# One margin, two passes and small random ranks in the list scheduler of a decoder block (gMLP gate, Conformer convolution, SwiGLU)

## The chip, the cores and the metric

The kernel runs on one core of a Trainium2 chip. The metric is the device time of one execution in microseconds (us), as the median of several runs. Lower is better.

## What is computed

One decoder block on 1024 tokens of width 1024, in float32, ends in a modulated RMSNorm:

```python
def reference(x, c, ...):
    c_act = jax.nn.silu(c)
    cond = c_act @ ada_w[i] + ada_b[i]          # six vectors: shift, scale, gate, twice
    h = modulate(rmsnorm(x, norm1_g[i]), shift1, scale1)
    u, v, val, gate = jnp.split(h @ w_in[i] + b_in[i], ...)
    y_a = spatial_gating_mixer(gelu(u), gelu(v), ...)      # causal within chunks of 128
    y_b = conformer_conv_mixer(val, gate, ...)             # 31 taps, group norm, silu
    y = jnp.concatenate([rmsnorm(y_a, ...), rmsnorm(y_b, ...)], axis=-1)
    x = x + gate1 * (y @ w_out[i])
    h2 = modulate(rmsnorm(x, norm2_g[i]), shift2, scale2)
    g_ff, up_ff = jnp.split(h2 @ w_ffn_in[i], 2, axis=-1)
    x = x + gate2 * ((jax.nn.silu(g_ff) * up_ff) @ w_ffn_out[i])
    return modulate(rmsnorm(x, norm_f_g), shift_f, scale_f)
```

## The kernel before

**Tiling.** Features lie on the 128 partitions, tokens on the free axis, in two halves of 512 tokens (half 0 and half 1). A matrix operand is split into a high and a low part (`wh_`, `wl_` for weights, the two planes of `h`), and `mm3` (L750 to L752) multiplies high by high, low by high and high by low, 128x512 each. The feed-forward products (L1139) do the same, in a seven-product scheme on blocks (names A, B and C for the accumulators).

**Stages on TensorE.** The projections of half 0 (`p`, `pu`), then of half 1 (`p10_0`, `p11_0`), the projection v of half 0 (`v0_0` to `v0_3`) and of half 1 (`v1_`), with the group norm (`gn`) and the gate of the mixer (`pm`) of half 0 in between, the rest of half 1, the output projection (`po`), products of the feed-forward made ahead (`ah`), and then the feed-forward up and down to the final norm.

**What the other engines do meanwhile.** VectorE (DVE) runs the depthwise convolution tap by tap into two PSUM banks: L1073 begins one (`cv`), L1070 adds a tap, L1079 adds the sum to `s`. It also makes the conditioning columns: L703 multiplies one 128x1024 piece of `ada_w` by the activated c and sums it (ada23 is such a piece, `ada_1041` in the order below; ada36 to ada39 are later ones). GpSimd (POOL) makes the low parts of weights (L734), other pieces of the conditioning (L700, with the sum at L701 on ScalarE) and adds taps that ScalarE has multiplied (L1065).

**Places that the prediction names.**
- L858 and L860: TensorE sums the spatial weights into the PSUM bank `rs`, and four DVE instructions at L860 read it into `bst`. `rs` is one of three banks with the tag `mm`; `v0_0` takes it next, so TensorE's first L750 of `v0_0` waits for the last L860.
- L1101, L687, L1114, L1115: the group norm. A reciprocal (L1101), four DVE instructions at L687 that spread it on a diagonal (`gd`; L684 on ScalarE before them), two matmuls (L1114), and the product at L1115 on DVE. gd00 is the one of the first pair of channel blocks of half 0, gd01 that of the second pair.
- L1013, L1017, L1019: the mixer. Eight small matmuls each for `pm0_0` to `pm0_3` and `pm1_0` to `pm1_3`; DVE finishes each at L1017 and L1019. These use the two banks with the tag `gn`, so `pm1_0` and `pm1_1` wait for L1115 of the second pair, and `pm1_2` waits for L1019 of `pm1_0`.
- L795, L799, L805: sums of squares, their reciprocal root and its broadcast (`ssq_a0`, `rt_a0`; `ssq_b0`, `rt_b0`).
- L1242 to L1247, L1267 to L1281, L1131 and L1132: preparing the feed-forward's operands.

**What sets the order.** `block_kernel` writes the program once. At its end, `fix_order` (L561) reads all instructions, and a list scheduler decides the order of each engine's instructions; the order is then fixed by dependencies without semaphores between neighbours. Each engine runs its list strictly in that order. `duration` (L144) has a duration for each instruction, `Clock` (L337) a model of the engines, the DMA queue, TensorE's clock and one shared port of DVE and POOL. `forward` (L397) walks through time and gives each free engine the ready instruction of the lowest rank; `backward` (L456) does the same from the end and gives each step its tail, the time from its start to the end of the program; the negative tail is the rank of the next forward pass. `stretched` multiplies the durations of steps off TensorE by the first number of a margin, and the bytes of transfers by the second. Before, three margins with four rounds of backward and forward give twelve orders. `replay` runs a given order through the same model; `jittered` does so with durations that are stretched at random, and `fix_order` keeps the order with the smallest sum of four such replays.

Of the kernel before, what the change touches and what calls it, by code (L numbers as in the profile page):

```python
# [67 lines left out]
ENGINES = ("PE", "DVE", "Activation", "Pool", "SP")  # L68
SIGNAL = {"PE": 0.043, "DVE": 0.024, "Activation": 0.024, "Pool": 0.068, "SP": 0.05}
# [5 lines left out]
DMA_AHEAD = 0.5  # L75
SHORT_ROWS = 1.15
CLOCK_WINDOW = 3.4133
MARGINS = ((1.01, 1.05), (1.015, 1.075), (1.02, 1.1))
JITTER = (0.008, 0.08)
TRIALS = 4  # L80


class Step:
# [313 lines left out]
def forward(g, rank):  # L397

    import heapq
    count = len(g.steps)  # L400
    need, at = [len(s.before) for s in g.steps], [0.0] * count
    done, order = [0.0] * count, {e: [] for e in ENGINES}
    ready, waiting = ({e: [] for e in ENGINES} for _ in range(2))
    parked = {tag: [] for tag in g.order}
    slots, clock, table = Slots(g), Clock(True), None

    def arrive(n):
        tag, t = slots.blocked_on(g.steps[n])
        if tag is not None:
            parked[tag].append(n)  # L410
            return
        heapq.heappush(waiting[g.steps[n].engine], (max(at[n], t), n))

    def wake(tags):
        for tag in tags:
            again, parked[tag] = parked[tag], []
            for n in again:
                arrive(n)

    for s in g.steps:  # L420
        if not need[s.n]:
            arrive(s.n)
    for _ in range(count):
        t, e = pick(clock, ready, waiting)
        while waiting[e] and waiting[e][0][0] <= t + 1e-6:
            n = heapq.heappop(waiting[e])[1]
            heapq.heappush(ready[e], (rank[n], n))
        chosen = ready[e][0]
        if e == "Activation" and g.steps[chosen[1]].table not in (None, table):
            others = [x for x in ready[e] if g.steps[x[1]].table in (None, table)]  # L430
            if others and min(others)[0] < chosen[0] + TABLE_LOAD:
                chosen = min(others)
        ready[e].remove(chosen)
        heapq.heapify(ready[e])
        s = g.steps[chosen[1]]
        woken = slots.take(s)
        if s.table not in (None, table):
            table, t = s.table, t + TABLE_LOAD
        begin, end = clock.run(s, t)
        done[s.n] = end  # L440
        order[e].append(s)
        woken += slots.release(s, end + SIGNAL[e])
        woken += slots.hand_over() if woken else []
        wake(woken)
        for n in s.after:
            need[n] -= 1
            same = g.steps[n].engine == e and not s.dma
            if (s.n, n) in g.turns:
                at[n] = max(at[n], t + DMA_ISSUE)
            else:  # L450
                at[n] = max(at[n], (clock.free[e] if e == "PE" else end) if same else end + SIGNAL[e])
            if not need[n]:
                arrive(n)
    return order, done, slots.follows


def backward(g, rank, follows):

    import heapq
    count = len(g.steps)  # L460
    before = [sorted(s.before) for s in g.steps]
    need, at, tail = [len(s.after) for s in g.steps], [0.0] * count, [0.0] * count
    for old, new in follows:
        for n in g.first[new]:
            for m in g.final[old]:
                if m != n:
                    before[n].append(m)
                    need[m] += 1
    ready, waiting = ({e: [] for e in ENGINES} for _ in range(2))
    clock = Clock()  # L470
    for s in g.steps:
        if not need[s.n]:
            heapq.heappush(waiting[s.engine], (0.0, s.n))
    for _ in range(count):
        t, e = pick(clock, ready, waiting)
        while waiting[e] and waiting[e][0][0] <= t + 1e-6:
            n = heapq.heappop(waiting[e])[1]
            heapq.heappush(ready[e], (rank[n], n))
        s = g.steps[heapq.heappop(ready[e])[1]]
        if s.dma:  # L480
            begin = max(t, clock.queue)
            clock.queue = begin + s.bytes / (LOAD_RATE if s.load else STORE_RATE) + LOAD_GAP
            end = clock.queue - LOAD_GAP + (LOAD_WAIT if s.load else STORE_WAIT)
            clock.free[e] = t + DMA_ISSUE
        else:
            begin, end = clock.run(s, t)
        tail[s.n] = end
        for n in before[s.n]:
            need[n] -= 1
            other = g.steps[n].engine  # L490
            if (n, s.n) in g.turns:
                at[n] = max(at[n], begin + DMA_ISSUE)
                if not need[n]:
                    heapq.heappush(waiting[other], (at[n], n))
                continue
            at[n] = max(at[n], begin + s.issue - (s.finish - s.issue) if other == e == "PE" else end + SIGNAL[other])
            if not need[n]:
                heapq.heappush(waiting[other], (at[n], n))
    return tail


def replay(g, order):

    place, done, at = dict.fromkeys(ENGINES, 0), {}, [0.0] * len(g.steps)
    need = [len(s.before) for s in g.steps]
    slots, clock, table = Slots(g), Clock(True), None
    for _ in range(len(g.steps)):
        best = None
        for e in ENGINES:
            if place[e] == len(order[e]) or need[order[e][place[e]].n]:  # L510
                continue
            s = order[e][place[e]]
            tag, t = slots.blocked_on(s)
            t = max(t, at[s.n], clock.free[e])
            if tag is None and (best is None or t < best[0]):
                best = t, s
        t, s = best
        slots.take(s)
        if s.table not in (None, table):
            table, t = s.table, t + TABLE_LOAD  # L520
        begin, end = clock.run(s, t)
        done[s.n] = end
        if slots.release(s, end + SIGNAL[s.engine]):
            slots.hand_over()
        for n in s.after:
            need[n] -= 1
            if (s.n, n) in g.turns:
                at[n] = max(at[n], t + DMA_ISSUE)
            elif g.steps[n].engine == s.engine and not s.dma:
                at[n] = max(at[n], clock.free["PE"] if s.engine == "PE" else end)  # L530
            else:
                at[n] = max(at[n], end + SIGNAL[s.engine])
        place[s.engine] += 1
    return max(done.values())


@contextmanager
def stretched(g, factor):

    kept = [(s, s.issue, s.finish, s.port, s.dma and s.bytes) for s in g.steps if s.engine != "PE"]  # L540
    for s, issue, finish, port, size in kept:
        f = factor(s)
        if s.dma:
            s.bytes = size * f
        else:
            s.issue, s.finish, s.port = issue * f, finish * f, port * f
    yield
    for s, s.issue, s.finish, s.port, size in kept:
        if s.dma:
            s.bytes = size  # L550


def jittered(g, order, seed):

    import random
    rng = random.Random(seed)
    with stretched(g, lambda s: 1 + abs(rng.gauss(0, JITTER[s.dma]))):
        return replay(g, order)


def fix_order(tc, edges, stacked, reusing, rounds=4):  # L561

    g = Graph(list(tc.nc.cur_bb.bb.instructions), edges, stacked, reusing)
    orders = []
    for margin in MARGINS:
        with stretched(g, lambda s: margin[s.dma]):
            order, done, follows = forward(g, list(range(len(g.steps))))
            for _ in range(rounds):
                tail = backward(g, [-t for t in done], follows)
                order, done, follows = forward(g, [-t for t in tail])  # L570
                orders.append(order)
    times = [sum(jittered(g, order, seed) for seed in range(TRIALS)) for order in orders]
    best = orders[times.index(min(times))]
    for steps in best.values():
        for earlier, later in zip(steps, steps[1:]):
            tc.add_manual_dep(later.ins, earlier.ins.name,
                              mybir.DependencyInfo(mybir.DependencyClass.NoSync, mybir.DependencyReason.DATA),
                              reason="fix_order")
# [1067 lines left out]
```

## Time and profile before

| | us |
|---|---|
| median of 3 runs | 964.54 |
| lowest and highest run | 963.92, 966.73 |
| the profiled execution's own time | 967.9 |
| its span, first to last instruction | 965.8 |

The profiled execution is 3.4 us above the median, and 2.1 us of it lie outside the span. Times in rows below are counted from the span's start. In a timeline row stand the start, the duration (of the whole group where it ends in xN), the engine and line, the operation with output and inputs (buffer numbers left out) and, in brackets, the idle time before it and what ended that. In a table by windows stand the busy time of each engine and its instructions, the granted TensorE clock as a share of full speed (PEclk), and the DMA engines' share and rate.

### The profile page before, as it was taken

The page shows a single profiled execution, that of the slowest core. Times are in us where ns is not written, and L with a number is a line of the kernel's source. Part 1 is how long each engine was busy: PE and PEld are TensorE (multiplying, and loading weights), DVE is VectorE, ACT ScalarE, POOL GpSimd, SP SyncE. Part 2 cuts the span into 40 slices and gives each one's busy share as a digit, 9 for nine tenths or more (in the row PEclk, how much of TensorE's full clock was granted, in tenths as well). Part 3 has the DMA queues.
Part 4 walks back from the last instruction along what each step waited for, and adds up shares of the span by engine and source line. Part 5 has one row for each costly group of instructions (what it writes and reads, how often), then busy time and mean ns, then how long its engine had stood idle before and what let it go on. Part 6 is the DMA issues. An engine that isn't in the chain of part 4 may idle for free.

```text
span 965.8 us, 12863 instructions
## 1 busy us (share of the span) xinstructions
PE 946.5 (98%) x4461; PEld 767.1 (79%) x4461; DVE 861.9 (89%) x1226; ACT 482.1 (50%) x770; POOL 413.6 (43%) x253
## 2 busy tenths in 40 slices
PE   7999999999999999999999999999999999999996
PEld 4888777778777788887888888888888888888885
DVE  6989999999999763899999999999778989969966
ACT  6778468763474743554333333223337337227426
POOL 0069896776554403673545454554534200000132
PEclk9999999999999999999999999999999999999998
DMA  9873342443385443753677677767648848405104
GB/s 351 325 265 136 110 174 88 153 159 130 139 280 202 147 146 138 263 205 119 239 238 251 221 236 243 249 236 238 224 171 277 269 158 260 164 33 165 54 1 174
DMA packets 70498, 184.24 MB, mean 191 GB/s; under 512 B 7841, under 2 KB 8353, under 8 KB 70434
## 3 DMA queue, kind: packets, MB, share of 16 engines
q1 hardware_dynamic: 70434, 183.43, 55.0%
q8 instruction: 35, 0.57, 0.3%
q14 instruction: 29, 0.24, 0.1%
HBM read 142.24 MB, written 41.16 MB: 190 GB/s over the span
## 4 chain that ended last, share of the span: by engine, by line
PE 84%; DVE 9%; DMA 2%; ACT 2%; issue 2%; POOL 1%; SPq 0%; POOLq 0%; ACTq 0%; DVEq 0%
PE B L1139 31%; PE C L1139 18%; PE ah L1139 9%; PE A L1139 3%; PE po L752 3%; PE po L751 3%; PE po L750 3%; DVE cv L1070 2%; PE p L752 2%; PE p L750 2%; PE p L751 2%; PE v L750 2%; PE v L752 1%; DVE ada L703 1%; PE v L751 1%
## 5 line engine op out<-in xcount | busy, mean ns | idle before, releaser
L1139 PE MATMUL B<-h,w_f 128*128 128x512 f32 x816 | 189.9, 389 | 0.6 <-ACT w_f L1131 0.3
L1139 PEld LDWEIGHTS B<-h,w_f 128*128 128x128 f32 x816 | 153.1, 188 | 33.0 <-ACT w_f L1131 0.8
L1070 DVE SCALAR_TENSOR_TENSOR cv<-ypad,colt,cv 128x512 f32<-128x512 f32 x216 | 147.8, 745 | 0.3
L1139 PE MATMUL B<-fa,w_d 128*128 128x512 f32 x528 | 125.0, 389 | 0.0
L1139 PE MATMUL C<-h,w_f 128*128 128x512 f32 x528 | 123.7, 389 | 0.0
L1139 PEld LDWEIGHTS C<-h,w_f 128*128 128x128 f32 x528 | 99.1, 188 | 20.9 <-ACT w_f L1131 0.3
L1139 PEld LDWEIGHTS B<-fa,w_d 128*128 128x128 f32 x528 | 99.0, 188 | 20.9 <-DVE x L1500 0.3
L1139 PE MATMUL ah<-h,wh_a 128*128 128x512 f32 x320 | 101.3, 394 | 0.0
L1426 POOL TENSOR_TENSOR sq_nf<-sq_nf,sq_nf 128x512 f32<-128x512 f32 (+1 forms) x15 | 17.4, 1163 | 170.9 <-ACT sq_nf L1420 170.8
L1131 ACT ACTIVATE w_f<-raw_f 128x512 fp32r<-128x512 f32 x68 | 42.4, 630 | 87.8 <-PE B L1139 38.8
L734 POOL TENSOR_TENSOR wl_a<-raw_a,wh_a 128x1024 fp32r<-128x1024 f32 x20 | 49.4, 2468 | 77.0 <-ACT wh_a L733 77.0
L1131 ACT ACTIVATE w_d<-raw_d 128x512 fp32r<-128x512 f32 (+1 forms) x72 | 42.0, 593 | 80.2 <-PE B L1139 33.6
L1132 DVE TENSOR_TENSOR w_f<-raw_f,w_f 128x512 fp32r<-128x512 f32 x68 | 71.7, 1061 | 7.6 <-ACT w_f L1131 7.4
L1139 PEld LDWEIGHTS ah<-h,wh_a 128*128 128x128 f32 x320 | 59.8, 188 | 14.8 <-issue 1.7
L1383 POOL TENSOR_TENSOR x<-x,up 128x512 f32<-128x512 f32 x20 | 36.1, 1805 | 73.4 <-ACT x L1382 73.4
L1139 PE MATMUL C<-fa,w_d 128*128 128x512 f32 (+1 forms) x291 | 63.9, 370 | 0.0
L1139 PE MATMUL ah<-h,wl_a 128*128 128x512 f32 x160 | 62.3, 389 | 0.0
L1139 PEld LDWEIGHTS C<-fa,w_d 128*128 128x128 f32 x291 | 51.0, 188 | 9.2
L1132 DVE TENSOR_TENSOR fa<-a,fa 128x512 fp32r<-128x512 f32 x77 | 52.0, 712 | 1.1 <-ACT fa L1131 1.1
L1500 DVE SCALAR_TENSOR_TENSOR x<-B,cond,x 128x512 f32<-128x512 f32 x48 | 35.7, 746 | 18.0 <-PE B L1139 17.5
L1132 DVE TENSOR_TENSOR w_d<-raw_d,w_d 128x512 fp32r<-128x512 f32 (+1 forms) x72 | 50.6, 712 | 0.0
L1131 ACT ACTIVATE fa<-a 128x512 fp32r<-128x512 f32 x77 | 46.5, 626 | 7.4 <-DMA a<-acts 4.8
(271 smaller groups left out, 2106.3 us busy)
## 6 DMA issues: line engine op xcount, KB each, us to landing
acts<-x SPq DMA_DIRECT2D x77, 256.0 KB, 3.3
a<-acts SPq DMA_DIRECT2D x77, 256.0 KB, 4.0
raw_f<-wf SPq DMA_DIRECT2D x32, 512.0 KB, 4.8
ada<-ada SPq DMA_DIRECT2D x24, 512.0 KB, 3.4
x<-ada SPq DMA_DIRECT2D x24, 512.0 KB, 4.0
raw_a<-wf SPq DMA_DIRECT2D x20, 512.0 KB, 3.3
ahead<-ahead SPq DMA_DIRECT2D x40, 256.0 KB, 2.5
ypad<-ada SPq DMA_DIRECT2D x16, 512.0 KB, 6.0
```

Of the source, the lines that this page charges most:

```text
L703: V.scalar_tensor_tensor(raw, raw, 1.0, cact, op0=ALU.mult, op1=ALU.mult, accum_out=cond[:, j:j + 1])
L734: lo_eng.tensor_tensor(lo[:, cut], raw[:, cut], hi[:, cut].bitcast(F32), op=ALU.subtract)
L750: PE.matmul(acc, shi, mhi, start=start, stop=False)
L751: PE.matmul(acc, slo, mhi, start=False, stop=False)
L752: PE.matmul(acc, shi, mlo, start=False, stop=stop)
L1070: V.scalar_tensor_tensor(accs[j], src, wc, accs[j], op0=ALU.mult, op1=ALU.add)
L1131: A.activation(dst[:, 0, :], src, AF.Copy)
L1132: lo_eng.tensor_tensor(dst[:, 1, :], src, dst[:, 0, :].bitcast(F32), op=ALU.subtract)
L1139: last_mm = PE.matmul(bank[:, cols], s, m[:, cols], start=first and p == 0 and i == 0, stop=p == n - 1 and i == 2, skip_group_check=True)
L1383: G.tensor_tensor(g0, g0, up0, op=ALU.mult)
L1426: G.tensor_tensor(run, run, t, op=ALU.add)
L1500: V.scalar_tensor_tensor(x_tile(k, part), bank[:, cols], ccol(GATE2, k), x_tile(k, part), op0=ALU.mult, op1=ALU.add)
```

## The change

The three margins become one, 1.03 off TensorE and 1.1 on transfers (before at most 1.02 and 1.1). The rounds go from four to two, and the rank of each forward pass after the first is the negative tail plus a random term with a standard deviation of 0.05 us from a fixed seed. The last order is used; `replay`, `jittered` and the choice among twelve are gone. The instructions themselves are the same, and every line of the kernel's body stands 47 lines earlier (L703 before is L656 after, L860 is L813, L1115 is L1068).

```diff
-MARGINS = ((1.01, 1.05), (1.015, 1.075), (1.02, 1.1))
-JITTER = (0.008, 0.08)
-TRIALS = 4
+MARGIN = (1.03, 1.1)
+ROUNDS_OF_ORDER, SPREAD, SEED = 2, 0.05, 807952
...
-def replay(g, order):
...
-def jittered(g, order, seed):
+def fix_order(tc, edges, stacked, reusing):
 
     import random
-    rng = random.Random(seed)
-    with stretched(g, lambda s: 1 + abs(rng.gauss(0, JITTER[s.dma]))):
-        return replay(g, order)
-
-
-def fix_order(tc, edges, stacked, reusing, rounds=4):
-
+    rng = random.Random(SEED)
     g = Graph(list(tc.nc.cur_bb.bb.instructions), edges, stacked, reusing)
-    orders = []
-    for margin in MARGINS:
-        with stretched(g, lambda s: margin[s.dma]):
-            order, done, follows = forward(g, list(range(len(g.steps))))
-            for _ in range(rounds):
-                tail = backward(g, [-t for t in done], follows)
-                order, done, follows = forward(g, [-t for t in tail])
-                orders.append(order)
-    times = [sum(jittered(g, order, seed) for seed in range(TRIALS)) for order in orders]
-    best = orders[times.index(min(times))]
-    for steps in best.values():
+    with stretched(g, lambda s: MARGIN[s.dma]):
+        order, done, follows = forward(g, list(range(len(g.steps))))
+        for _ in range(ROUNDS_OF_ORDER):
+            tail = backward(g, [-t for t in done], follows)
+            order, done, follows = forward(g, [-(t + rng.gauss(0, SPREAD)) for t in tail])
+    for steps in order.values():
```

Three places on DVE follow, each before and after. The first is around ada23 (`ada_1041`), while TensorE works on `p10_0` and `p11_0`. Before:

```order
L703 SCALAR_TENSOR_TENSOR ada_1041,cond<-ada_1041,cact 128x1024
L1070 SCALAR_TENSOR_TENSOR cv_0_1214<-ypad_108,colt,cv_0_1214 128x512
L1070 SCALAR_TENSOR_TENSOR cv_1_1215<-ypad_109,colt,cv_1_1215 128x512
...
L1070 SCALAR_TENSOR_TENSOR cv_1_1215<-ypad_109,colt,cv_1_1215 128x512
L1079 TENSOR_TENSOR s_0_1210<-s_0_1210,cv_0_1214 128x512
L1079 TENSOR_TENSOR s_1_1211<-s_1_1211,cv_1_1215 128x512
L1073 TENSOR_SCALAR cv_2_1530<-ypad_110,colt 128x512
L1073 TENSOR_SCALAR cv_3_1531<-ypad_111,colt 128x512
L860 SCALAR_TENSOR_TENSOR bst<-rs,colt,bst 128x128 x4
```

The same place on DVE after the change (L656 is L703, L813 is L860, L1023 is L1070, L1032 is L1079 of before):

```order
L1023 SCALAR_TENSOR_TENSOR cv_0_1214<-ypad_108,colt,cv_0_1214 128x512
L656 SCALAR_TENSOR_TENSOR ada_1041,cond<-ada_1041,cact 128x1024
L813 SCALAR_TENSOR_TENSOR bst<-rs,colt,bst 128x128 x4
L1023 SCALAR_TENSOR_TENSOR cv_1_1215<-ypad_109,colt,cv_1_1215 128x512
L1023 SCALAR_TENSOR_TENSOR cv_0_1214<-ypad_108,colt,cv_0_1214 128x512
L1023 SCALAR_TENSOR_TENSOR cv_1_1215<-ypad_109,colt,cv_1_1215 128x512
L1032 TENSOR_TENSOR s_0_1210<-s_0_1210,cv_0_1214 128x512
```

Before, eight taps, two sums and two first taps stood between ada23 and the four instructions that free the bank `rs`. After, these four follow ada23 at once, and five taps that followed ada23 stand ahead of it.

The second place is the first group norm on DVE (`gd_1321` is gd00). Before:

```order
L1101 RECIPROCAL gsd_0_1318<-gsd_0_1318 128x128
L985 SCALAR_TENSOR_TENSOR nb_1204<-mv_1022,sd_1023 128x4
L1070 SCALAR_TENSOR_TENSOR cv_2_1530<-ypad_110,colt,cv_2_1530 128x512
L687 SCALAR_TENSOR_TENSOR gd_1321<-gd_1321,colt,gsd_0_1318 32x128 x4
L1070 SCALAR_TENSOR_TENSOR cv_3_1531<-ypad_111,colt,cv_3_1531 128x512
L1115 TENSOR_TENSOR s_0_1210<-s_0_1210,gn_1_1301 128x512
```

And after (L640 is L687, L1054 is L1101, L1068 is L1115):

```order
L1054 RECIPROCAL gsd_0_1318<-gsd_0_1318 128x128
L936 RECIPROCAL sd_1023<-sd_1023 128x4
L1023 SCALAR_TENSOR_TENSOR cv_2_1530<-ypad_110,colt,cv_2_1530 128x512
L938 SCALAR_TENSOR_TENSOR nb_1204<-mv_1022,sd_1023 128x4
L1023 SCALAR_TENSOR_TENSOR cv_3_1531<-ypad_111,colt,cv_3_1531 128x512
L640 SCALAR_TENSOR_TENSOR gd_1321<-gd_1321,colt,gsd_0_1318 32x128 x4
L1023 SCALAR_TENSOR_TENSOR cv_2_1530<-ypad_110,colt,cv_2_1530 128x512
L1023 SCALAR_TENSOR_TENSOR cv_3_1531<-ypad_111,colt,cv_3_1531 128x512
L1068 TENSOR_TENSOR s_0_1210<-s_0_1210,gn_1_1301 128x512
```

One tap more stands ahead of gd00's four instructions, and one more between them and L1115. On TensorE, the two matmuls at L1114 that read gd00 stand two matmuls of `v1_2` earlier than before.

The third place is the second group norm on DVE, up to the `pm` of half 1 (`gd_1637` is gd01, `ada_1861` is ada36, `ada_1895` is ada37, `ada_1932` is ada38). Before:

```order
L1026 SCALAR_TENSOR_TENSOR yn_a_0_1674<-ya_0_594,colt,ssq_a_1651 128x512
L687 SCALAR_TENSOR_TENSOR gd_1637<-gd_1637,colt,gsd_1_1634 32x128 x4
L1026 SCALAR_TENSOR_TENSOR yn_a_1_1679<-ya_0_594,colt,ssq_a_1651 128x512
L1026 SCALAR_TENSOR_TENSOR yn_a_2_1684<-ya_1_595,colt,ssq_a_1651 128x512
L1115 TENSOR_TENSOR s_2_1212<-s_2_1212,gn_3_1617 128x512
L1115 TENSOR_TENSOR s_3_1213<-s_3_1213,gn_2_1616 128x512
L1026 SCALAR_TENSOR_TENSOR yn_a_3_1689<-ya_1_595,colt,ssq_a_1651 128x512
L703 SCALAR_TENSOR_TENSOR ada_1895,cond<-ada_1895,cact 128x1024
L703 SCALAR_TENSOR_TENSOR ada_1932,cond<-ada_1932,cact 128x1024
L1017 SCALAR_TENSOR_TENSOR pm_0_1694<-pm_0_1694,colt,bst 128x512
```

And after (L979 is L1026, L970 is L1017):

```order
L640 SCALAR_TENSOR_TENSOR gd_1637<-gd_1637,colt,gsd_1_1634 32x128 x4
L656 SCALAR_TENSOR_TENSOR ada_1861,cond<-ada_1861,cact 128x1024
L979 SCALAR_TENSOR_TENSOR yn_a_0_1674<-ya_0_594,colt,ssq_a_1651 128x512
L979 SCALAR_TENSOR_TENSOR yn_a_1_1679<-ya_0_594,colt,ssq_a_1651 128x512
L979 SCALAR_TENSOR_TENSOR yn_a_2_1684<-ya_1_595,colt,ssq_a_1651 128x512
L979 SCALAR_TENSOR_TENSOR yn_a_3_1689<-ya_1_595,colt,ssq_a_1651 128x512
L656 SCALAR_TENSOR_TENSOR ada_1895,cond<-ada_1895,cact 128x1024
L1023 SCALAR_TENSOR_TENSOR cv_0_2869<-ypad_108,colt,cv_0_2869 128x512
L1068 TENSOR_TENSOR s_2_1212<-s_2_1212,gn_3_1617 128x512
L1068 TENSOR_TENSOR s_3_1213<-s_3_1213,gn_2_1616 128x512
L1023 SCALAR_TENSOR_TENSOR cv_0_2869<-ypad_108,colt,cv_0_2869 128x512 x2
L656 SCALAR_TENSOR_TENSOR ada_1932,cond<-ada_1932,cact 128x1024
```

The last yn_a and ada37 now stand ahead of the two L1115, and one tap that stood ahead of them now stands behind. On TensorE, `pm1_0` stands three matmuls later than before, `pm1_2` one later, and the broadcast at L805 that reads `rt_b0` six later; on DVE, the end of `pm1_0` and `pm1_1` (L1019) has one tap more ahead of it, and `rt_b0` has three.

31 lines of the change are left out of this document (removed).

## The prediction, made before the run

> **What bounds the kernel now.** I read the page's busy shares first, then a table by windows, then TensorE's waits, then timelines around the longest of them.
>
> ```profile
> PE 946.5 (98%) x4461; PEld 767.1 (79%) x4461; DVE 861.9 (89%) x1226; ACT 482.1 (50%) x770; POOL 413.6 (43%) x253
> ```
>
> TensorE is busy 98% of the span, so a new order can win only the rest. The windows tell where that rest lies:
>
> ```profile
> 13.00:119.00 106.00, 103.33 (x486) 83.35 (x486) 100.28 (x138) 71.95 (x109) 56.47 (x33) 1.00 0.64 231
> 119.00:122.00 3.00, 0.88 (x4) 0.46 (x3) 3.00 (x8) 2.97 (x5) 3.00 (x2) 1.00 0.41 135
> 122.00:126.00 4.00, 4.00 (x12) 3.12 (x11) 4.00 (x7) 1.81 (x3) 4.00 (x4) 0.58 0.62 216
> 126.00:200.00 74.00, 73.24 (x435) 57.64 (x436) 73.09 (x114) 57.46 (x91) 59.84 (x36) 1.00 0.38 133
> 200.00:250.00 50.00, 49.45 (x243) 39.91 (x239) 50.00 (x75) 22.19 (x28) 32.28 (x20) 1.00 0.40 140
> 250.00:446.00 196.00, 195.19 (x924) 154.47 (x923) 159.21 (x216) 109.40 (x165) 89.57 (x46) 1.00 0.53 186
> 446.00:728.00 282.00, 282.00 (x1246) 233.49 (x1245) 265.89 (x339) 92.47 (x151) 138.56 (x88) 1.00 0.67 229
> 728.00:945.00 217.00, 217.00 (x966) 179.60 (x965) 185.61 (x288) 101.30 (x177) 23.89 (x15) 1.00 0.45 149
> ```
>
> From 446 to 945 the first column of busy time (TensorE) fills both windows: 499 us in which an order can only lose. From 119 to 446 TensorE is idle 2.12 + 0.76 + 0.55 + 0.81 = 4.24 us, half of it in the three microseconds after 119, and right behind that the clock column falls to 0.58. DVE, the third column, is full from 119 to 250 (3.00 of 3.00, 4.00 of 4.00, 73.09 of 74, 50.00 of 50). So there are two bounds at once: TensorE nearly everywhere, and DVE close behind from 119 to 250. The waits name the longest of those places and the last (the two between them stand in rows further down):
>
> ```profile
> PE v L750 <- DVE bst L860: 2.1, 1, 2.1
> PE gn L1114 <- DVE late L687: 0.2, 1, 0.2
> ```
>
> **The stall at 119 and what it cost.** DVE, then POOL, then TensorE around it:
>
> ```profile
> 106.15 6.59 DVE L703 SCALAR_TENSOR_TENSOR ada<-ada,cact 128x1024 f32<-128x1024 f32 x1
> 112.67 5.36 DVE L1070 SCALAR_TENSOR_TENSOR cv<-ypad,colt,cv 128x512 f32<-128x512 f32 x8
> 117.94 1.27 DVE L1079 TENSOR_TENSOR s<-s,cv 128x512 f32<-128x512 f32 x2
> 120.44 1.11 DVE L860 SCALAR_TENSOR_TENSOR bst<-rs,colt,bst 128x128 f32<-128x128 f32 x4
> ```
>
> ```profile
> 106.90 4.76 POOL L734 TENSOR_TENSOR wl_v<-raw_v,wh_v 128x1024 fp32r<-128x1024 f32 x2
> 123.28 2.42 POOL L734 TENSOR_TENSOR wl_v<-raw_v,wh_v 128x1024 fp32r<-128x1024 f32 x1
> ```
>
> ```profile
> L703 DVE SCALAR_TENSOR_TENSOR ada<-ada,cact x12: 1211/1914/6586, 49.0 to 199.1; 128x1024 f32<-128x1024 f32 x12
> ```
>
> ```profile
> 116.70 0.39 PE L750 MATMUL p<-h,wh_vg 128*128 128x512 f32 x1
> 119.19 0.39 PE L752 MATMUL p<-h,wh_vg 128*128 128x512 f32 x1
> 121.70 0.47 PE L750 MATMUL v<-wh_v,h 128*128 128x512 f32 x1 [2.12 <-DVE bst L860]
> 126.11 0.39 PE L750 MATMUL v<-wh_v,h 128*128 128x512 f32 x1
> ```
>
> ada23 took 6.59 us on DVE; the shortest of the twelve pieces of this kind took 1.211 (the row has minimum, median and maximum in ns). It ended at 112.74, 1.1 us after POOL's two wl_v (106.90 + 4.76 = 111.66): DVE seems to be held off while POOL runs back to back, and to do its own work after it. Eight taps, two sums and two first taps later, L860 freed the bank for TensorE, which starts a matmul each 0.227 us (11 intervals from 116.70 to 119.19, rounded up). It was due at 119.42 and began at 121.70: 2.28 us. The 12 intervals from there to 126.11 took 4.41 us instead of 2.72, which is the window with the low clock: 1.69 us. The stall cost **3.97 us**.
>
> The Trainium skill, SBUF — State Buffer, Who interferes with whom, says that a DVE instruction with two SBUF inputs and a GpSimd instruction that reads SBUF exclude each other, and the one that starts first holds its port for the whole instruction; ada23 agrees (6.59 against 1.211 us), and by that rule any reordering may make new such pairs. The Trainium skill, TensorE: Matmul & The Clock Gate, What's actually happening, lets the clock fall after an idle window of about 3.4 us; here it fell after 2.12 us of idleness, so the measurement decides. [...]
>
> **The change, term by term.** Five taps now run ahead of ada23, at 5.27/8 = 0.66 us each (112.67 to 117.94), so it starts at 106.15 + 3.30 = 109.45, is held until 111.66 as before, and ends at about the same 112.75. L860 follows at once and ends at 113.9, 5.5 us ahead of need. What is late next is the low part of v's last weights: POOL ended it at 123.28 + 2.42 = 125.70, and TensorE will need it 24 matmuls after 119.42, at 124.87. If nothing moves on POOL, 0.83 is lost; but the pieces ahead of it there wait for ScalarE and for transfers that now start behind wl_v and no longer behind ada23, so I take the other end, 0, for a term of **-3.97**. DVE itself wins the five taps, 3.30, less the 0.08 by which ada23 ends later: a lead of 3.22 us. That is less than TensorE's 3.97, and where TensorE waits for DVE with more rows ahead, the difference is paid back.
>
> ```profile
> 154.26 5.84 DVE L687 SCALAR_TENSOR_TENSOR gd<-gd,colt,gsd 32x128 fp32r<-32x128 f32 x4
> 187.62 1.42 DVE L687 SCALAR_TENSOR_TENSOR gd<-gd,colt,gsd 32x128 fp32r<-32x128 f32 x4
> ```
>
> ```profile
> 157.29 6.44 POOL L1065 TENSOR_TENSOR s<-s,cp 128x512 f32<-128x512 f32 x5
> 190.80 2.54 POOL L1029 TENSOR_TENSOR y_a<-yn_a,y_a 128x512 fp32r<-128x512 f32 x2 [4.34 <-ACT y_a L1028]
> ```
>
> ```profile
> 160.52 0.62 PE L1114 MATMUL gn<-gd 128*128 128x512 f32 x2
> ```
>
> *gd00.* Its four instructions took 5.84 us beside a busy POOL, and 1.42 for gd01 while POOL sat idle. TensorE is now due at L1114 at 160.52 - 3.97 - 2 x 0.227 = 156.10. If the four still take 5.84, they end at 160.10 - 3.22 + 0.66 (one tap more ahead) = 157.54: a wait of **+1.44**. If they find POOL idle, 4.42 us sooner: 0. If one waits for a POOL piece of 2.4 us more, about 3.9. I take 1.44, the row of the same four instructions.
>
> ```profile
> 190.39 1.28 DVE L1115 TENSOR_TENSOR s<-s,gn 128x512 f32<-128x512 f32 x2
> 191.58 0.74 DVE L1026 SCALAR_TENSOR_TENSOR yn_a<-ya,colt,ssq_a 128x512 f32<-128x512 f32 x1
> 192.24 2.18 DVE L703 SCALAR_TENSOR_TENSOR ada<-ada,cact 128x1024 f32<-128x1024 f32 x1
> 197.91 1.27 DVE L1019 TENSOR_TENSOR ya<-ya,pm 128x512 f32<-128x512 f32 x2
> 208.24 0.94 DVE L799 RECIPROCAL rt_b<-rt_b 128x128 f32<-128x128 f32 x1
> ```
>
> ```profile
> 192.60 1.97 PE L1013 MATMUL pm<-wt,vn 128*64 128x128 f32 x32
> 197.58 0.39 PE L752 MATMUL p<-h,wh_vg 128*128 128x512 f32 x1
> 198.73 1.97 PE L1013 MATMUL pm<-wt,vn 128*64 128x128 f32 x32 [0.76 <-DVE ya L1019]
> 208.29 0.39 PE L751 MATMUL p<-h,wl_vg 128*128 128x512 f32 x1
> 209.24 1.16 PE L805 MATMUL ssq_b<-rt_b,sel_tok 128*128 128x128 f32 x8 [0.56 <-DVE rt_b L799]
> 210.15 0.48 PE L752 MATMUL p<-h,wh_vg 128*128 128x512 f32 x1
> 210.47 0.40 PE L750 MATMUL po<-y_a,wh_o 128*128 128x512 f32 x1
> ```
>
> TensorE's lead is then 2.53. *pm1_0*: L1115 now has yn_a (0.66) and ada37 (2.11) more and a tap (0.66) less ahead: 191.67 - 3.22 + 2.11 = 190.56; TensorE is due at 192.60 + 3 x 0.227 - 2.53 = 190.75: **0**. *pm1_2*: DVE's L1019 ends at 199.18 - 3.22 + 0.66 = 196.62; TensorE is due at 197.81 + 0.23 - 2.53 = 195.51, a wait of 1.11 against 0.92 before (198.73 less 197.81): **+0.19**. *rt_b0*: DVE ends at 209.18 - 3.22 + 3 x 0.66 = 207.94, TensorE is due at 208.52 + 6 x 0.227 - 2.34 = 207.54, a wait of 0.40 against 0.72 before: **-0.32**. The lead is 2.66.
>
> *Smaller ones.* The sums of squares of half 1 (53 to 59 us) come in two pieces more; each return to large matmuls costs about 0.1 (210.15 to 210.47 against 0.227) and each entry as much, so +0.3. The 0.2 at L1114 of a later group norm goes, since its chain stands earlier. From 384 to 446, one ada piece moves out of DVE's way and two operands of the first feed-forward tile come later; between a loss of 2 and the gain of the waits there (at most the 0.81 of that window) I take 0. Behind 446 TensorE is full and its operands were ready; the tail's order is nearly the same: 0.
>
> Sum: -3.97 + 1.44 + 0 + 0.19 - 0.32 + 0.3 - 0.2 = **-2.56**. On the profiled execution's own time, 967.9 becomes 965.3. That execution stands 3.4 above the median of 964.54; I move the median by the same amount: **962.0**.
>
> **The rivals.**
> - *More is kept.* The four at gd00 find POOL idle, the later waits go too. Everything idle from 119 to 446 and the clock's 1.69 is 5.9 us, so down to 958.6; about 960 is likely (-3.97 and a few tenths of the later waits). For it: gd01's 1.42. Against: POOL was busy for 6.44 us in that stretch for reasons that the order leaves standing.
> - *Slower: a DVE piece is held off ahead of L1115.* ada36 and ada37 now both stand between gd01 and the L1115 for which `pm1_0` waits, with POOL splitting weights then. ada37 took 2.18; held like ada23 it takes 6.59, 4.4 more, and if ada36 is held too, 4.4 again at most. L1115 then ends at 195.0, TensorE waits 4.2, and such a wait costs 1.69 of clock: -2.56 + 4.2 + 1.7 = +3.3, or 967.9; with both held 972. It decides from the point where L1115 ends later than 193.3, 2.7 us more than I have it. Against: it needs two POOL pieces back to back at that moment, as only one of the twelve ada pieces met.
> - *Nothing is left.* The payback at gd00 is 3.9, or the entry to the feed-forward loses 2: within 1.5 us of 964.5. This includes the change not doing what it says: if L860 were still late, only where it waits would differ.
>
> **How the numbers follow.** A measurement of this kernel can tell about 0.3%, 2.9 us, from no change. My forecast, -1 to -4, has 0.46, of which 0.20 lie beyond 2.9; more kept 0.22; nothing left 0.10; slower by a held piece 0.22. Faster: 0.20 + 0.22 = 0.42. Same: 0.26 + 0.10 = 0.36. Slower: 0.22. The range of 958.6 to 968.0 reaches from the full gain to one held piece, and leaves out the double one and part of the others. Both signs are likely enough that the forecast's own range, 960.5 to 963.5, stands beside it.
>
> **What would show it.** Right: no wait of `v0_0` for L860, clock 1.00 from 119 to 126, ada23 near 3.3 us, a wait of 1 to 2 us at L1114 near 156, waits near 1.1 and 0.4 at `pm1_2` and L805. Wrong: another L703 or L687 held for over 4 us ahead of an awaited instruction, a second window below full clock, a wait for weights in `v0_0`, or idle TensorE behind 446.

## The result, and the profile after

| | before | after |
|---|---|---|
| median of 18 runs each on one chip (lowest to highest) | 966.61 us (963.77 to 969.1) | 962.33 us (961.73 to 964.2) |
| after over before, 95% interval | | 0.996 (0.9951 to 0.9969), so 3.9 us less (3.0 to 4.7) |
| profiled execution, its own time | 967.9 us | 962.08 us |
| its span | 965.8 us | 959.8 us |

The changed kernel is faster, and 962.33 stands 0.3 from the 962.0 forecast. Two things deserve a look before that is taken for understanding. The kernel before spreads over 5.3 us from run to run, the kernel after over 2.5. And the profiled executions differ by 5.8, more than the medians (4.28), since before's is one of its slower runs and after's one of its faster.

The busy shares of the page of after:

```profile
PE 944.2 (98%) x4461; PEld 766.6 (80%) x4461; DVE 863.2 (90%) x1226; ACT 482.0 (50%) x770; POOL 408.7 (43%) x253
```

They tell next to nothing: the same work, the same shares. The table by windows of after, cut where the prediction cut before's (columns of busy time: TensorE, its weight loads, DVE, ACT, POOL; then clock, DMA share, GB/s):

```profile
13.00:119.00 106.00, 103.35 (x483) 82.78 (x484) 98.32 (x144) 73.04 (x110) 59.49 (x35) 1.00 0.65 232
119.00:122.00 3.00, 3.00 (x15) 2.49 (x14) 3.00 (x6) 1.95 (x2) 2.99 (x2) 1.00 0.90 288
122.00:126.00 4.00, 4.00 (x20) 3.30 (x19) 4.00 (x7) 2.15 (x5) 4.00 (x3) 1.00 0.26 74
126.00:200.00 74.00, 74.00 (x450) 58.06 (x449) 72.59 (x118) 61.26 (x95) 63.41 (x37) 1.00 0.43 147
200.00:250.00 50.00, 50.00 (x244) 40.74 (x244) 49.26 (x75) 19.74 (x26) 28.99 (x19) 1.00 0.39 136
250.00:446.00 196.00, 195.97 (x918) 156.53 (x917) 161.43 (x215) 112.55 (x172) 86.55 (x45) 1.00 0.55 188
```

TensorE's column is full from 119 to 446 but for 0.03 us, where 4.24 stood idle before, and the clock from 122 to 126 is 1.00 and no longer 0.58. The 4.24 less 0.03 and the clock's 1.69 make 5.9, near the 6.0 by which the span is shorter. The two are not the same thing, as the table further down shows: the stretch gave 7.4, and 0.64 was lost ahead of it and some more behind it. All of TensorE's waits in after that the view lists:

```profile
PE c L615 <- DMA c_row<-c: 2.3, 1, 2.3
PE p L703 <- ACT h L881: 1.7, 1, 1.7
PE ssq_nf L1397 <- DVE rt_nf L1395: 1.6, 1, 1.6
PE ssq_n L850 <- DVE rt_n L848: 1.1, 1, 1.1
PE p L705 <- DVE h L886: 1.0, 1, 1.0
PE ssq_nf L1365 <- POOL sq_nf L1379: 0.4, 1, 0.4
PE ssq_n L843 <- ACT sq_n L841: 0.2, 1, 0.2
```

None lies between 119 and 446; these are the program's start and its tail. So not only the wait for L860 is gone (L813 now), but also the two of 0.76 and 0.56 near 199 and 209.

To see when each microsecond came, I set the two traces side by side, matmul for matmul, and noted by how much after is ahead:

| at, in us of after | what is new there | ahead by |
|---|---|---|
| 95 to 119 | more pieces in the sums of squares, 71 to 82 us (0.49 of it) | -0.64 |
| 120 | `v0_0` starts without a wait | +1.64 |
| 124 | the low clock is gone | +3.35 |
| 157 | L1067 (L1114 before), gd00: nothing paid back | 3.4 |
| 195 | `pm1_2` does not wait | 4.2 |
| 204 | L758 (L805 before) does not wait for `rt_b0` | 5.0 |
| 325 to 330 | the later group norm: +0.55 | 5.8 |
| 437 to 439 (443 to 446 before) | first operands of the feed-forward part: +0.9 | 6.7 |
| end | -0.3 near 618, then small change | 6.3 |

The last figure is counted at the last matched matmul and stands 0.3 above the difference of the spans. From 119 to 446 it goes from -0.64 to 6.7, which is 1.5 more than idle time and clock. Part of that shows beside the waits, where matmuls also follow each other more slowly (in before's trace 0.52 us apart at 444.16, against 0.227). So the 5.9 was no upper bound on what an order can win there.

### The profile page after: what moved, and what is told of

It is laid out like the page before. It is cut to its first block, busy times and chain, and to the rows that moved or that the text cites. A ratio compares the mean times of both kernels' runs of the same rounds, so it can differ in the third digit from the quotient of the medians.

```text
span 959.8 us, 12886 instructions
## 1 busy us (share of the span) xinstructions
PE 944.2 (98%) x4461; PEld 766.6 (80%) x4461; DVE 863.2 (90%) x1226; ACT 482.0 (50%) x770; POOL 408.7 (43%) x253
## 4 chain that ended last, share of the span: by engine, by line
PE 97%; DVE 2%; DMA 1%; ACT 0%; SPq 0%; issue 0%; ACTq 0%; DVEq 0%
PE B L1092 32%; PE C L1092 19%; PE ah L1092 11%; PE A L1092 4%; PE po L705 3%; PE po L704 3%; PE po L703 3%; PE p L705 3%; PE p L704 3%; PE p L703 3%; PE pu L705 2%; PE v L704 2%; PE v L703 2%; PE pu L703 2%; PE v L705 2%; PE pu L704 2%
## 5 line engine op out<-in xcount | busy, mean ns | idle before, releaser
L1023 DVE SCALAR_TENSOR_TENSOR cv<-ypad,colt,cv 128x512 f32<-128x512 f32 x216 | 147.8, 745 | 0.5
L687 POOL TENSOR_TENSOR wl_a<-raw_a,wh_a 128x1024 fp32r<-128x1024 f32 x20 | 49.0, 2456 | 77.7 <-ACT wh_a L686 77.7
L1085 DVE TENSOR_TENSOR w_f<-raw_f,w_f 128x512 fp32r<-128x512 f32 x68 | 68.5, 1016 | 1.3 <-ACT w_f L1084 1.3
L1339 POOL TENSOR_TENSOR x<-x,u 128x512 f32<-128x512 f32 x22 | 35.8, 1627 | 52.8 <-DVE u L1338 52.8
L1336 POOL TENSOR_TENSOR x<-x,up 128x512 f32<-128x512 f32 x20 | 31.7, 1586 | 42.2 <-ACT x L1335 42.2
```

What stands on the lines that cost most here:

```text
L687: lo_eng.tensor_tensor(lo[:, cut], raw[:, cut], hi[:, cut].bitcast(F32), op=ALU.subtract)
L1023: V.scalar_tensor_tensor(accs[j], src, wc, accs[j], op0=ALU.mult, op1=ALU.add)
L1085: lo_eng.tensor_tensor(dst[:, 1, :], src, dst[:, 0, :].bitcast(F32), op=ALU.subtract)
L1336: G.tensor_tensor(g0, g0, up0, op=ALU.mult)
L1339: G.tensor_tensor(g1, g1, u2, op=ALU.mult)
```

## The experiments

Each experiment's effect is taken against runs of the kernel before on the same chip. In code that the edits lengthen, lines shift: L716, L669 and L671 are before's L703 and after's L656, and L873, L828 and L826 are L860 and L813; in the two splices every line stands 45 later than in before. The theories on trial: that `ada23`, held by POOL, is what costs (A); that L860's late place alone is what costs (B); that the rest of the new order carries part of the gain (C); that the part of the order ahead of 260 us carries it (D) or the part behind carries half (E); and that the hold comes out differently from run to run (F) or the spread has another source (G).

### L860 early, and nothing else

The kernel before, with DVE's four `bst` instructions put right behind `ada23`:

```diff
+    best["DVE"] = moved(best["DVE"], "bst", "rs", lambda rest: 1 + max(
+        i for i, s in enumerate(rest) if named(s, "ada23")))
```

> The kernel before, with one edit: on VectorE the four instructions at L860 stand right behind ada23. Theory A (two bounds): the wait of 2.1 us and the low clock at 119 go, worth 4.0 us there, but VectorE has won nothing, so TensorE waits for gd00 about 3.5 us at L1114 and for the places behind it: 0 to 1 us faster than before in all. Theory B (the bank alone): nothing else waits for these four, so the 4 us stay: 3.5 to 4.5 us faster.

966.87 us median of 12 runs (963.72 to 969.2), before 967.18 of 31 (963.86 to 969.98): 0.9997 (0.9981 to 1.0013). Nothing is gained, so the late place of L860 is not by itself what costs. Where the runs with a long hold then lose their time was not caught in a profile: the profiled run, 963.83 us, is among the quickest, and it shows something else. Its DVE, then its POOL:

```profile
106.07 1.87 DVE L716 SCALAR_TENSOR_TENSOR ada<-ada,cact 128x1024 f32<-128x1024 f32 x1
...
108.44 1.13 DVE L873 SCALAR_TENSOR_TENSOR bst<-rs,colt,bst 128x128 f32<-128x128 f32 x4 [0.49 <-PE rs L871]
```

```profile
105.56 1.29 POOL L1078 TENSOR_TENSOR s<-s,cp 128x512 f32<-128x512 f32 x1
106.81 5.74 POOL L747 TENSOR_TENSOR wl_v<-raw_v,wh_v 128x1024 fp32r<-128x1024 f32 x2
```

And POOL in before, one instruction ahead of the pair that the prediction shows:

```profile
105.65 1.31 POOL L1065 TENSOR_TENSOR s<-s,cp 128x512 f32<-128x512 f32 x1
```

`ada23` starts at the same place as in before, 0.74 us ahead of POOL's two `wl_v`, but takes 1.87 instead of 6.59, and it is POOL's two that take a microsecond longer: 5.74 instead of 4.76. Nothing ahead of `ada23` was edited. In both executions POOL is still adding a tap (L1065, here L1078) when `ada23` starts, so DVE has to wait for that. When POOL changes to its next instruction, near 106.9, DVE got in here (`ada23` ends 1.09 us later), and in before POOL went on, through both `wl_v`.

### `ada23` later, L860 where it was

The kernel before, with `ada23` five instructions later on DVE, behind the taps that the change also puts ahead of it:

```diff
+    best["DVE"] = moved(best["DVE"], "ada23", "", lambda rest: 5 + next(
+        i for i, s in enumerate(best["DVE"]) if named(s, "ada23")))
```

> The kernel before, with one edit: ada23 stands five taps later on VectorE, and L860 stays where it was, behind the first taps. Theory A: the five taps run while GpSimd holds ada23 off anyway, VectorE leads by 3.2 us, L860 ends near 118.3 where TensorE needs it at 119.4, no wait there, and the lead pays at the later waits: 3 to 5 us faster. Theory B (the place of the four alone counts): L860 still stands behind all the taps, and at most the part of the wait goes that ada23's hold made: 0 to 2 us faster.

964.61 us of 12 runs (963.32 to 966.21), 0.9973 (0.996 to 0.9986), so 2.6 us less (1.4 to 3.9) than the same 31 runs: between what the two theories gave, and no verdict between them.

```profile
111.15 3.29 DVE L716 SCALAR_TENSOR_TENSOR ada<-ada,cact 128x1024 f32<-128x1024 f32 x1
...
118.85 1.11 DVE L873 SCALAR_TENSOR_TENSOR bst<-rs,colt,bst 128x128 f32<-128x128 f32 x4
```

L873 stands as late in the order as before and still ends at 119.96, soon enough: TensorE waits for it nowhere. The waits of 0.7 and 0.6 at `pm1_2` and `rt_b0` remain. `ada23` began inside the second `wl_v` and waited for the rest of that one only. So a shorter hold suffices, without moving L860.

### The kernel after, with `ada23` five earlier

```diff
+    order["DVE"] = moved(order["DVE"], "ada23", "", lambda rest: next(
+        i for i, s in enumerate(order["DVE"]) if named(s, "ada23")) - 5)
```

> The kernel after, with one edit: ada23 stands five taps earlier, as in before; L860 follows the five taps. L860 ends near 118, still ahead of TensorE's 120. Theory A: VectorE loses 3.2 us, so no wait at 119, but waits of 2 to 3 us at L1114 near 157 and more behind: 2 to 4 us slower than after, level with before or up to 2 us faster. Theory B: no change against after.

962.94 us of 8 runs (960.94 to 963.88), 0.9953 (0.9935 to 0.9972): not slower than the change itself. The expected hold did not come about, so the run decides nothing between A and B. Here `ada23`, then POOL:

```profile
107.84 1.34 DVE L669 SCALAR_TENSOR_TENSOR ada<-ada,cact 128x1024 f32<-128x1024 f32 x1
```

```profile
105.68 2.42 POOL L700 TENSOR_TENSOR wl_vg<-raw_vg,wh_vg 128x1024 fp32r<-128x1024 f32 x1
108.04 2.29 POOL L1031 TENSOR_TENSOR s<-s,cp 128x512 f32<-128x512 f32 x1
110.29 4.76 POOL L700 TENSOR_TENSOR wl_v<-raw_v,wh_v 128x1024 fp32r<-128x1024 f32 x2
```

It met POOL two instructions ahead of the pair, got in at the first change, near 108.1, and ended at 109.18, and POOL's next instruction took 2.29 us where it takes 1.32 in after. POOL began its pair at 110.29, 2.5 us later than in after, about 1 us of which `ada23` itself caused. A place in DVE's order fixes no meeting with POOL: POOL's own times shift, and with them the instruction that is met. This miss is what made me look at the meeting and no longer at the place.

### The kernel after, with both put back as before

```diff
+    order["DVE"] = moved(order["DVE"], "bst", "rs", lambda rest: 1 + min(
+        i for i, s in enumerate(rest) if named(s, "cv0_3")))
+    order["DVE"] = moved(order["DVE"], "ada23", "", lambda rest: next(
+        i for i, s in enumerate(order["DVE"]) if named(s, "ada23")) - 5)
```

> The kernel after, with VectorE's order around ada23 and L860 put back to that of before (all else as after). Both theories: the wait and the low clock at 119 come back, 3 to 4.5 us slower than after. If it is level with before, this place is the whole change; what is left is what the rest of the new order is worth. Rival C (the rest of the order carries part of it): it stays 1 to 2 us faster than before.

964.05 us of 12 runs (962.32 to 968.89), 0.9973 (0.9956 to 0.999), so about 2.6 us less than before (1.0 to 4.3), with the stall's place as in before. Its DVE, its POOL, the wait and the window behind it:

```profile
105.88 7.27 DVE L671 SCALAR_TENSOR_TENSOR ada<-ada,cact 128x1024 f32<-128x1024 f32 x1
...
120.85 1.12 DVE L828 SCALAR_TENSOR_TENSOR bst<-rs,colt,bst 128x128 f32<-128x128 f32 x4
```

```profile
107.31 4.75 POOL L702 TENSOR_TENSOR wl_v<-raw_v,wh_v 128x1024 fp32r<-128x1024 f32 x2
```

```profile
PE v L718 <- DVE bst L828: 2.4, 1, 2.4
```

```profile
122.00:126.00 4.00, 3.88 (x11) 3.11 (x12) 4.00 (x7) 2.94 (x4) 4.00 (x2) 0.59 0.75 252
```

The profiled run (965.26) has the whole stall back: hold, late L828, wait, half clock. None of the other waits between 126 and 446 is there. Its span of 962.9 us is 3.1 above that of after, as both theories gave; the median is not 3 to 4.5 above after's but about 1.3 by the ratios, with intervals that overlap. So this place can bring the stall back, and the rest of the new order wins about 2.6 us on its own, which is rival C, with more than its 1 to 2 us. The profiles agree, stall against stall: 962.9 is 2.9 below before's span of 965.8. Four of the 12 runs lie at 962.3 to 962.7, as quick as the change itself; the others reach up to 968.9. Its spread of 6.6 us is like before's (6.1 there): with the order in that place, the spread comes back.

### Half of the new order

Both orders, spliced near 260 us: first the new one ahead of the splice and the old behind it, then the reverse.

```diff
-    best = orders[times.index(min(times))]
...
+    early, late = order_after(g), order_before(g)
...
+    for e in ENGINES:
+        order[e] = early[e][:cut[e]] + late[e][cut[e]:]
```

> A splice: each engine runs the order of after up to about 260 us of the run and the order of before behind that (the cut stands where both orders have the same set of instructions behind them). Theory D (the first 260 us carry the gain: the place of ada23 and L860, and the waits at pm1_2 and rt_b0 that are gone, 5.0 us in the two profiles): within 2 us of after, with waits of 0.2 to 0.9 us back near 333 and 443. Rival E (the later places, 333 and 443, and what follows them carry half): 2 to 3 us slower than after.

970.38 us of 12 runs (966.74 to 971.76), 1.0014 (1.0001 to 1.0026) against 968.28 of 23. Neither forecast came about, and the run is inconclusive. Up to the splice it is about 4.2 us ahead of before, without a wait at `v0_0`. But the splice makes a wait of its own, the longest of all:

```profile
PE ah L1184 <- ACT ahead L1199: 3.0, 1, 3.0
```

```profile
284.00:290.00 6.00, 3.41 (x9) 2.74 (x10) 3.43 (x6) 3.97 (x7) 6.00 (x4) 0.77 0.66 229
```

It costs 3.0 and about 1.7 of clock behind it, which is the whole of the gain. The total says nothing of either order.

```diff
+    early, late = order_before(g), order_after(g)
```

> The splice the other way: before up to about 260 us, after behind that. Theory D: 0.5 to 1.7 us faster than before, with its runs spread as widely as those of before (964 to 969). Rival E: 2 to 3 us faster.

967.32 us of 11 runs (965.37 to 968.67), 0.9987 (0.9975 to 0.9999), so 1.3 us less (0.1 to 2.4), which is what D gave, though the interval reaches into what E gave. TensorE's waits keep those of before ahead of the splice:

```profile
PE v L795 <- DVE bst L905: 2.1, 1, 2.1
...
PE pm L1058 <- DVE ya L1064: 0.7, 1, 0.7
PE ssq_b L850 <- DVE rt_b L844: 0.6, 1, 0.6
```

Against before's trace it wins about 0.6 near 330 and 0.9 near 445. So the places of the later group norm and of the first feed-forward operands are worth about 1.3 us together.

### Margin and draw

The random term switched off, and another seed:

```diff
-ROUNDS_OF_ORDER, SPREAD, SEED = 2, 0.05, 807952
+ROUNDS_OF_ORDER, SPREAD, SEED = 2, 0.0, 807952
```

> The kernel after, with the random term taken out of the ranks (a standard deviation of 0), margin and rounds as in after. If the margin makes the gain, it stays 3 to 5 us faster than before; if the draw of the random term does, it is within 2 us of before or slower.

```diff
-ROUNDS_OF_ORDER, SPREAD, SEED = 2, 0.05, 807952
+ROUNDS_OF_ORDER, SPREAD, SEED = 2, 0.05, 1
```

> The kernel after with another seed (1) of the random term. If the random term only breaks ties, it is within 1 us of after; if the order of after is one lucky draw of a wide set, it is 2 to 6 us slower than after.

963.93 us (963.33 to 964.42) and 964.18 us (963.74 to 965.49), 5 runs each: 0.9947 (0.9935 to 0.9959) and 0.9953 (0.9941 to 0.9965). Without the draw the gain is all there, and another draw keeps it, so it comes from the new margin, the two rounds and the dropped choice among twelve orders; no run takes these three apart. In the kernel without the draw, gd00 on DVE and TensorE, and then the one listed wait at L1067:

```profile
150.62 5.84 DVE L640 SCALAR_TENSOR_TENSOR gd<-gd,colt,gsd 32x128 fp32r<-32x128 f32 x4
```

```profile
157.11 0.62 PE L1067 MATMUL gn<-gd 128*128 128x512 f32 x2
...
330.35 0.47 PE L1067 MATMUL gn<-late 128*128 128x512 f32 x1 [0.71 <-DVE late L640]
```

gd00's four take 5.84 again, as before, and still end at 156.46, 0.65 us ahead of TensorE: no wait there. The wait of 0.7 is that of the later group norm (`late`), which is 0.2 in before and none in the change. The other seed has the same two things: 5.84 without a wait at gd00, and 0.7 at the later group norm. So the payback at gd00 that I had forecast is seen in neither.

### `ada23` past POOL's pair

In the kernel before and in the kernel after, `ada23` eight instructions later on DVE, to start when POOL's two are over:

```diff
+    best["DVE"] = moved(best["DVE"], "ada23", "", lambda rest: 8 + next(
+        i for i, s in enumerate(best["DVE"]) if named(s, "ada23")))
```

> The kernel before, with ada23 eight taps later on VectorE, where GpSimd has done its two wl_v and waits for a transfer; L860 keeps its place. Theory F (the hold of ada23, which comes out differently from run to run, makes both the cost and the spread of before): ada23 takes 1.2 to 1.6 us, no wait at L860, the time is that of the lowest runs of before, 2.5 to 4.5 us below its median, and the runs lie within 3 us. Rival G (the spread has another source and the hold's cost is paid back behind it): the spread stays 4 us or more, and the gain is 1.5 us or less.

```diff
+    order["DVE"] = moved(order["DVE"], "ada23", "", lambda rest: 8 + next(
+        i for i, s in enumerate(order["DVE"]) if named(s, "ada23")))
```

> The kernel after, with ada23 behind the four of L860, three taps and one sum, so that it starts when GpSimd idles. Theory F: ada23 takes 1.2 to 1.6 us instead of 4.0, VectorE gains 2.7 us there, but TensorE waits for nothing between 119 and 446 in after, so the time stays within 1 us of after (4 to 6 us faster than before). If VectorE's lead still counted, it would be 1.5 us or more faster than after.

The kernel before was profiled twice more, unchanged, to see whether the hold differs between its executions:

> The kernel before, unchanged, for a second profile. Theory F: ada23's duration differs or not, and the time goes with it: near 6.6 us and a wait at L860, 967 to 969 us; below 3 us and no wait there, 964 to 965 us. Rival G: the time does not follow ada23.

> The kernel before, unchanged, for a third profile, with the same expectation as the second: by theory F the time follows ada23's duration (near 6.6 us: 967 to 969; below 3 us: 964 to 965), by rival G it does not.

Before, in 9 runs there: 968.6 us (967.34 to 969.19). With `ada23` eight later in the old order 964.49 of 5 (963.77 to 965.46), 0.9958 (0.9944 to 0.9971); in the new order 962.23 of 5 (961.87 to 962.83), 0.9935 (0.9923 to 0.9948). Here `ada23` of the one, and POOL:

```profile
111.25 1.32 DVE L716 SCALAR_TENSOR_TENSOR ada<-ada,cact 128x1024 f32<-128x1024 f32 x1
```

```profile
106.75 4.75 POOL L747 TENSOR_TENSOR wl_v<-raw_v,wh_v 128x1024 fp32r<-128x1024 f32 x2
```

It meets only the last quarter of a microsecond of POOL's pair and takes 1.32. One piece moved by eight places gives 4.1 us, close to the 3.99 that the stall cost in the trace. All nine runs of before lie near the top of its range here, as the two profiled ones with their hold do; the spread of the two moved kernels is 1.7 us in the old order and 1.0 in the new. Since before itself spreads over only 1.9 us there, these runs do not test whether the hold makes the spread, the other half of theory F. The new order with this piece moved is the quickest of the study, 6.3 us under before on its chip. It was not timed beside the change on one chip, and its 962.23 is no different from the change's 962.33; that it beats the change is not shown.

The two further profiles of before, 968.4 and 967.87 us, both have the hold (6.58 and 6.59 us). A quick run of before itself was not caught in a profile. That its quick runs, down to 963.8, are those in which DVE gets in at the first change is an inference from the kernel with L860 early, whose order is the same up to and with `ada23`.

## Why the prediction was right, and where its terms were off

**The stall at 119: right, and to the size.** -3.97 was forecast, and the side-by-side has 3.99: after goes from 0.64 behind to 3.35 ahead between 119 and 124. Its parts came as described: DVE in after, then POOL.

```profile
109.68 4.00 DVE L656 SCALAR_TENSOR_TENSOR ada<-ada,cact 128x1024 f32<-128x1024 f32 x1
...
113.61 1.11 DVE L813 SCALAR_TENSOR_TENSOR bst<-rs,colt,bst 128x128 f32<-128x128 f32 x4
```

```profile
107.83 4.77 POOL L687 TENSOR_TENSOR wl_v<-raw_v,wh_v 128x1024 fp32r<-128x1024 f32 x2
121.17 2.41 POOL L687 TENSOR_TENSOR wl_v<-raw_v,wh_v 128x1024 fp32r<-128x1024 f32 x1
```

`ada23` began at 109.68 (forecast 109.45), was held to POOL's end at 112.60 (forecast 111.66) and ended at 113.68 (112.75). v's last low part came at 123.58, 2.1 us sooner than before, so the end that I took for it, 0, held. What the prediction did not see is that the hold is no constant of the order, and that in before POOL was already at L1065 when `ada23` began: its remark that `ada23` agrees with an exclusive port holds, but `ada23` was passed over at two changes of POOL's instruction, which it did not ask about. On medians the place is worth 1.3 us in the new order (0.996 against 0.9973 with both put back) and 2.6 or 4.1 in the old one (five or eight places). These figures come from different chips, and their intervals overlap; the two moved kernels themselves lie at 964.61 and 964.49.

**The payback at gd00: mis-sized, 0 in place of +1.44.** DVE and TensorE in after:

```profile
151.02 4.83 DVE L640 SCALAR_TENSOR_TENSOR gd<-gd,colt,gsd 32x128 fp32r<-32x128 f32 x4
```

```profile
156.47 0.40 PE L926 MATMUL v<-vb,vsel 128*128 128x512 f32 x1
156.71 0.62 PE L1067 MATMUL gn<-gd 128*128 128x512 f32 x2
```

The four ended at 155.85 (forecast 157.54), and TensorE came to them at 156.71 (156.10), so the end was 0.86 early and not 1.44 late. Three things make up the 2.30 between: the four took 4.83 instead of 5.84 (1.01); they began at 151.02 and not at 151.70 (0.68), in a chain whose small L985 (L938 after) took 0.15 us and before 1.10; and TensorE led by 3.35 and not by 3.97, having lost 0.64 ahead of 119 (0.61). I had said that with POOL idle it would be 0; POOL was not idle, only less in the way. No run shows the payback itself: in none of the 14 profiles does TensorE wait for gd00, not even where the four take 5.84.

**The later waits: mis-sized, about -0.75 and -0.8 in place of +0.19 and -0.32.** They were forecast as 1.11 and 0.40 and are gone. The ada pieces 36 to 39 in after:

```profile
181.41 1.23 DVE L656 SCALAR_TENSOR_TENSOR ada<-ada,cact 128x1024 f32<-128x1024 f32 x1
...
185.19 2.20 DVE L656 SCALAR_TENSOR_TENSOR ada<-ada,cact 128x1024 f32<-128x1024 f32 x1
...
190.63 1.51 DVE L656 SCALAR_TENSOR_TENSOR ada<-ada,cact 128x1024 f32<-128x1024 f32 x1
...
194.58 2.14 DVE L656 SCALAR_TENSOR_TENSOR ada<-ada,cact 128x1024 f32<-128x1024 f32 x1
```

They took 7.08 us together, and 10.53 before (2.70, 2.18, 2.30, 3.35). I had carried before's durations over to the new order; a duration that is mostly hold does not carry over. The slower rival had asked for two POOL instructions back to back, and ada37 (at 185.19) did meet two:

```profile
185.02 3.54 POOL L982 TENSOR_TENSOR y_a<-yn_a,y_a 128x512 fp32r<-128x512 f32 x2
```

DVE got in between them; that is why POOL's two take 3.54 us, about 1 more than such a pair before (2.54), and ada37 only 2.20. In before, too, ada37 to ada39 each met POOL at such a change and got in, so the prediction's "only one of the twelve ada pieces met" two back to back was a misreading: only one of the twelve was passed over.

**The smaller ones.** The sums of squares cost 0.49 (forecast 0.3), at 71 to 82 us and not at 53 to 59. The later group norm gave 0.55 (0.2). The entry to the feed-forward part gave 0.9, where I took 0 between a loss of 2 and a gain of at most 0.81. The stretch behind 446 lost 0.3 where I took 0.

**The sum, and why it still fell right.** On the profiled execution's own time the terms gave -2.56, or 965.3; it was 962.08, so -5.8. By that measure the rival "more is kept" came about, down to what it took for the bound: everything idle and the clock's 1.69, which it put at 5.9. The other step that failed is the one by which I moved the median by the same amount. Before's profiled run was 3.4 above the median then at hand, probably because it had the hold and some other runs did not (not shown, since no quick run of before was profiled); the upper end of the runs fell by 4.9 us and the lower end by 2.0, and the median moved by 3.9 to 4.3. Too small a gain, on the low one of before's two medians (964.54 with 3 runs, 966.61 with 18), gave the right number. The direction, the place and the largest term on the profiled execution were right for the reasons given; that 962.0 was met to 0.3 us is partly luck.

What stays open: a quick execution of before in a profile, what decides whether `ada23` gets in, where L860 moved early loses its time when the hold is long, the worth of the first half of the order by itself (its splice spoiled it), and whether moving `ada23` on top of the change is worth anything.

## What to carry to other kernels

Where DVE and POOL are both busy, read the longest instance of a group against its shortest, and look at the other engine over exactly those microseconds: the excess belongs to the meeting, not to the instruction, and must not be carried over to a new order. When a kernel's runs spread more than its neighbours', look for such a meeting ahead of a wait; moving one instruction past it may give much of what a new schedule gives, as the 4.1 us here. Before a wait is counted for a theory, look at its time and its tile: one source line serves several places. And compare terms with the profiled execution, but say where that execution stands among the runs before the sum is put on a median.

## What the runs showed of the hardware

**Who gets in is not fixed by the order.** In the 14 profiles `ada23` takes 1.22 us where POOL is idle (once). In the other 13 it begins while POOL is at an instruction and ends 1.08 or 1.09 us behind the end of a POOL instruction; the question is which one. In two (3.29 and 1.32 us) POOL had nothing to go on with. In eight (before three times, after, both put back, both splices, without the draw) POOL went on at every change, for one to three more instructions, until it paused: 3.98 to 7.27 us. In three DVE got in at the first change, and POOL's next instruction took about 1 us longer: L860 early (1.87), `ada23` five earlier in the new order (1.34), and the other seed, here on DVE and POOL:

```profile
111.46 1.61 DVE L656 SCALAR_TENSOR_TENSOR ada<-ada,cact 128x1024 f32<-128x1024 f32 x1
```

```profile
109.60 5.73 POOL L687 TENSOR_TENSOR wl_v<-raw_v,wh_v 128x1024 fp32r<-128x1024 f32 x2
```

Here `ada23` began inside the first `wl_v` and got in between the two. So one of the two is kept out while the other works, and the loser can be kept out over several instructions of the winner. Of the twelve ada pieces in each of the 14 traces, a held piece met 115 changes of POOL's instruction; DVE got in at 101 of them, and all 14 others belong to `ada23`. What is different about it these runs do not show. The Trainium skill, SBUF — State Buffer, Who interferes with whom, calls the shared ports an exclusive lock, which these rows bear out; which side gets it at a change in a given execution, they leave open, since before and the kernel with L860 early have the same order up to there.

**The clock drops at small waits.** Waits of TensorE of 2.1 us (before, and the splice with the old order first), 2.4 (both put back) and 3.0 (the other splice) were each followed by some 3 to 4 us at about half clock, worth about 1.7 us. Waits up to 0.8 us between 119 and 446 showed no window under 1.00, and neither did the wait of 1.7 us near 15 us that every profile has.
